# One kernel, three edits: adaLN's later vectors summed along rows, w_out rounded on ScalarE, the output projection's store moved

## The chip, the cores and the metric

The kernel runs on one core of one Trainium2 chip. The metric is the device time of one execution in microseconds (us). Engines are named as the profile names them: PE is TensorE's matmul side and PEld its weight loads, DVE is VectorE, ACT is ScalarE, POOL is GpSimd, SP is SyncE, which here only issues transfers.

## What is computed

One layer of an encoder trunk with batch 1, sequence 1024 and width 1024, all in float32. A conditioning vector c gives six vectors of 1024 numbers (adaLN), which modulate the layer:

```python
mod = silu(c) @ w_ada + b_ada                      # 6 vectors: shift, scale, gate for each half
h = modulate(rms_norm(x), shift_mix, scale_mix)
proj = h @ w_in                                    # q, k, v of 8 + 8 heads of 64
oa = chunked_rel_attention(...)                    # 8 heads, a band of 9 chunks of 64
ob = stick_breaking_attention(...)                 # 8 heads, causal, cumulative products
x = x + gate_mix * (concat(rms_norm(oa) * g_a, rms_norm(ob) * g_b) @ w_out)
h = modulate(rms_norm(x), shift_ffn, scale_ffn)
gate, val = split(causal_depthwise_conv(h @ w_up))
x = x + gate_ffn * ((silu(gate) * val) @ w_down)   # then a last rms_norm
```

Vectors 0 and 1 (shift_mix, scale_mix) are needed at the start. The "later vectors" are 2 to 5: gate_mix for the output projection, shift_ffn and scale_ffn for the second half, gate_ffn for its last product.

## The kernel before, in words

Every float32 product is made of three products of rounded parts: each operand is split into a high part (the value rounded to fp32r) and a low part (the rest), and `mm3g` (L468) issues high by high, high by low, low by high.

The work has three stages: a prologue to about 60 us (rms_norm, vectors 0 and 1 by `ada_sum` at L250, the first q and k), the attention to about 640 us, and the feed-forward part to the end.

The attention is one list of 128 units (L939): 8 pairs of heads, 4 groups of queries, 2 heads, 2 blocks of 128 queries. Units 0 to 63 are stick-breaking: scores, two sigmoids, a scan on VectorE (L799), a product on POOL (L802). Units 64 to 127 are chunked attention: scores, a maximum on VectorE (L767, L771), exp on ScalarE (L778), normalisation on POOL (L795). Then TensorE transposes the probabilities (tile T from pb), ScalarE and VectorE split them (L821, L822), and TensorE multiplies them by v. The loop at L944 works two units ahead with the scores, and between these steps `fill` (L664) puts in matmuls of a list of jobs with due times (L609 to L652): the q, k and v projections of coming pairs, then `job_out_b` (L545), the half of the output projection that belongs to the stick-breaking heads, and two blocks of `job_out_a`. By the planner's costs and due times `job_out_b` begins in unit 106 and ends in unit 125.

At the end of each unit from MOD0 = 60 on (L48, L972) the loop takes one step of `mods` (L891). One step handles two tiles of w_ada, 128 inputs by 256 outputs each (tile rawm, four buffers, loads at L901). VectorE multiplies a tile by one value of silu(c) per partition and adds it to macc (L916, L918). There are 4 vectors by 4 quarters by 8 tiles, 128 tiles. After each eighth tile `mod_out` (L924) sums macc over the partitions with TensorE: for vectors 3 and 4 two products of macc by a column of ones (shown as T<-ones,macc), for the gates one product of ones by macc (T<-macc,ones), into a PSUM buffer that the transposes use too (T, three buffers). A gate's quarter gets its bias from a small load and is stored to the scratch gate_d, from where `load_gate` (L542) reads it back broadcast.

Four things set the order. TensorE's instructions are pinned to the order of the program (`pe`, L134 to L136). The other engines' instructions and SP's transfers are put in order by the framework's scheduler, which goes by program order and by its own model of when a thing is ready; each engine then runs its list strictly in that order, and an instruction that waits holds all behind it. All transfers are issued by SP. And a buffer is refilled only when its last reader is done.

`job_out_b` works on 16 blocks of 128 rows by 512 columns. For one block it loads the rows of x, issues 12 matmuls, scales the result on VectorE (L567), adds it to x on POOL (L568), and stores it to scratch tb_d (L569). `load_wout` (L516) loads a tile of w_out, rounds it on VectorE (L521) and takes the rest on POOL (L522); two buffers (raw) hold the loads. The lines around a block's end are:

```python
yield from mm3g(ps, out_prs(wo, ot, tb, hf, fbs), 216)      # L565
ve.scalar_tensor_tensor(st, ps, rB[:, tb:tb + 1], bc[:, cc], ALU.mult, ALU.mult)
gp.tensor_add(xt, xt, st)
sy.dma_start(tb_d[tb, :, cc], xt)                           # L569
```

`mm3g` gives control back after each matmul, the last one too; there is no such point between L566 and the next block's first matmul.

Of the kernel before, what the change touches and what calls it, by code (L numbers as in the profile page):

```python
# [47 lines left out]
MOD0 = 60  # L48
# [7 lines left out]
def build(nc, tc, t, ctx):  # L56
# [3 lines left out]
    def mk(pool, shape, dt, tag):  # L60
        cnt[0] += 1
        return pool.tile(shape, dt, name=f"{tag}_{cnt[0]}", tag=tag, bufs=BUFS.get(tag, 1))
# [16 lines left out]
    rev_d = mk(dr, [8, P, ULEN], F32, "revd")  # L79

# [54 lines left out]
    def pe(fn, *a, **k):  # L135
# [7 lines left out]
    smask = mk(pq, [P, P], F32, "smask")  # L143
    gp.memset(smask, 0.0)
    gp.affine_select(out=smask, in_=smask, pattern=[[-1, P]], compare_op=ALU.is_gt,
                     fill=NEG, base=0, channel_multiplier=1)
    smaskr, identr = (mk(pq, [P, P], F32R, n) for n in ("smaskr", "identr"))
    gp.tensor_copy(smaskr, smask)
# [69 lines left out]
    ada = t["ada0"]  # L218
    sh_mix = mk(p0, [P, KB], F32, "sh_mix")
# [235 lines left out]
    sy.dma_start(rev_d, bass.AP(t["rev"].tensor, 0, [[ULEN, 8], [0, P], [1, ULEN]]))  # L455
    new_k(pairs[0])
# [59 lines left out]
    def load_wout(kb, hf):  # L516
        cc = slice(hf * HALF, (hf + 1) * HALF)
        raw = load_w(t["w_out"][kb, :, cc], [P, HALF])
        wh = mk(pH, [P, HALF], F32R, "H")
        wl = mk(pH, [P, HALF], F32R, "H")  # L520
        ve.tensor_copy(wh, raw)  # L521
        gp.tensor_sub(wl, raw, f(wh))  # L522
        return wh, wl
# [21 lines left out]
    def job_out_b(_):  # L545
# [10 lines left out]
        bc = mk(p1, [P, S + 1], F32, "kt")  # L556
        load_gate(bc[:, 0:D])
        gate.append(bc)
        for hf in range(2):
            cc = slice(hf * HALF, (hf + 1) * HALF)  # L560
            for tb in range(TB):
                ps = mk(ps1, [P, HALF], F32, "mm")
                xt = mk(p0, [P, KB, P], F32, "wh").rearrange("p a b -> p (a b)")[:, 0:HALF]
                sy.dma_start(xt, t["x"][tb * P:(tb + 1) * P, cc])
                yield from mm3g(ps, out_prs(wo, ot, tb, hf, fbs), 216)  # L565
                st = mk(p0, [P, KB, P], F32, "wl").rearrange("p a b -> p (a b)")[:, 0:HALF]  # L566
                ve.scalar_tensor_tensor(st, ps, rB[:, tb:tb + 1], bc[:, cc], ALU.mult, ALU.mult)  # L567
                gp.tensor_add(xt, xt, st)  # L568
                sy.dma_start(tb_d[tb, :, cc], xt)  # L569
                if hf == 1 and tb == 3:  # L570
                    for fb in range(4):
                        ot[fb, 0] = load_o(fb, 0, fb < 3)
                    for fb in range(4):
                        wo[fb, 0] = load_wout(fb, 0)
        for fb in range(4):
            wo[fb, 1] = load_wout(fb, 1)
# [312 lines left out]
    QC = 256  # L889

    def mods():  # L891


        seq = [(i, qt, kb) for i in MODS for qt in range(D // QC) for kb in range(KB)]
        tiles = {}

        def load(n):
            if n < len(seq):
                i, qt, kb = seq[n]
                tiles[n] = mk(p1, [P, QC], F32, "rawm")  # L900
                sy.dma_start(tiles[n], t["ada"][i - 2, kb, :, qt * QC:(qt + 1) * QC])  # L901

        load(0)
        load(1)
        yield
        for n, (i, qt, kb) in enumerate(seq):
            cols = i in (3, 4)
            if n % 2 == 0:
                load(n + 2)
                load(n + 3)  # L910
            w = tiles.pop(n)
            if kb == 0:
                if cols and qt == 0:
                    modv[i] = mk(p0, [P, KB], F32, f"mod{i}")
                acc = mk(p1, [P, QC], F32, "macc")
                ve.tensor_scalar(acc, w, cact[:, 0:1], None, ALU.mult)  # L916
            else:
                ve.scalar_tensor_tensor(acc, w, cact[:, kb:kb + 1], acc, ALU.mult, ALU.add)  # L918
            if kb == KB - 1:
                mod_out(i, qt, acc, cols)  # L920
            if n % 2:
                yield

    def mod_out(i, qt, acc, cols):  # L924
        mp = mk(ps1, [P, HALF], F32, "T")
        if cols:
            for b in range(2):
                pe(te.matmul, mp[:, b:b + 1], acc[:, b * P:(b + 1) * P], ones[:, 0:1], start=True, stop=True)
            k0 = 2 * qt
            ve.scalar_tensor_tensor(modv[i][:, k0:k0 + 2], mp[:, 0:2], 0.0 if i == 3 else 1.0,  # L930
                                    bada[:, 8 * i + k0:8 * i + k0 + 2], ALU.add, ALU.add)
        else:
            pe(te.matmul, mp[:, 0:QC], ones, acc, start=True, stop=True)
            bb = mk(p1, [1, QC], F32, "rawm")
            sy.dma_start(bb, bass.AP(t["b_ada"].tensor, i * D + qt * QC, [[QC, 1], [1, QC]]))
            ve.tensor_add(acc[0:1], mp[0:1, 0:QC], bb)
            sy.dma_start(gate_d[i // 5:i // 5 + 1, qt * QC:(qt + 1) * QC], acc[0:1])
# [583 lines left out]
```

## Time and profile before

| | us |
|---|---|
| median of 3 runs | 1426.35 |
| lowest and highest run | 1421.34, 1428.23 |
| the profiled execution, its own time | 1425.51 |
| its span, first to last instruction | 1423.5 |
| busy in it: PE, DVE, POOL, ACT | 1309.2, 1176.2, 864.9, 617.2 |

The profile is one execution, recorded instruction by instruction. Busy time of an engine says how much it did, not whether the end waited for it. A wait is idle time of an engine together with what ended it. Matmuls are pipelined, so the time between the starts of two of them is less than the duration shown. PEclk is the TensorE clock that was granted, as a share of 2.4 GHz; its two levels are 1.2 and 2.4 GHz, so 0.5 would be the lower level throughout.

### The profile page before, as it was taken

Reading aid. Unit: us, or ns where it says so; the run is one execution under the profiler, and the core shown is the slowest. Engines: PE = TensorE matmul, PEld = TensorE weight load, DVE = VectorE, ACT = ScalarE, POOL = GpSimd, SP = SyncE. Lnnn points to the kernel's source line nnn. Section 1 sums busy time; section 2 is a strip of 40 time slices with the busy share of each in tenths; the row PEclk is TensorE's granted clock in tenths of the full one; section 3 lists DMA queues with packets and bytes.
Section 4 is the critical chain, followed back from the end, with each engine's and each line's share of the span. In section 5 each row is a group of like instructions: output and inputs, shape, how many; then the busy total and the mean of one; then the engine's idle time right before and its main releaser. Section 6 shows DMA issues by size and latency. Waiting matters only on the chain.

```text
span 1423.5 us, 19845 instructions
## 1 busy us (share of the span) xinstructions
PE 1309.2 (92%) x6644; PEld 1083.0 (76%) x6644; DVE 1176.2 (83%) x1967; ACT 617.2 (43%) x1270; POOL 864.9 (61%) x760
## 2 busy tenths in 40 slices
PE   4889999999899978798887999999999999999996
PEld 2688998898778966676665877777777778777774
DVE  7858777677778868876889889999998889899887
ACT  5647567575545433333432333323333333333334
POOL 4646576765333436563578667776676677667664
PEclk9999999999999999899998999999999999999998
DMA  8534433414665686665011111111111111211213
GB/s 311 180 100 112 104 88 85 119 49 120 166 167 144 179 263 197 217 193 193 22 45 36 47 52 45 45 45 60 52 54 58 45 45 45 60 52 49 62 37 119
DMA packets 80047, 144.57 MB, mean 102 GB/s; under 512 B 10041, under 2 KB 36809, under 8 KB 79946
## 3 DMA queue, kind: packets, MB, share of 16 engines
q1 hardware_dynamic: 79946, 143.31, 33.9%
q8 instruction: 53, 0.87, 0.3%
q14 instruction: 48, 0.39, 0.1%
HBM read 102.89 MB, written 18.88 MB: 86 GB/s over the span
## 4 chain that ended last, share of the span: by engine, by line
PE 43%; DVE 35%; ACT 7%; issue 5%; DMA 5%; POOL 4%; SPq 1%; POOLq 0%; DVEq 0%; ACTq 0%
PE mm L136 14%; PE up L1128 12%; DVE y L1137 8%; PE T L136 6%; PE dnf L136 6%; DVE x L1262 4%; PE S L136 3%; ACT y L1133 3%; DVE ah L1071 3%; DVE y L1070 2%; DVE adaw L254 1%; DVE macc L918 1%; PE up L1302 1%; POOL wl L121 1%; DVE al L1072 1%
## 5 line engine op out<-in xcount | busy, mean ns | idle before, releaser
L1262 DVE TENSOR_TENSOR x<-dnf,x 128x512 f32<-128x512 f32 x340 | 222.5, 679 | 1.6 <-PE dnf L136 1.6
L1137 DVE SCALAR_TENSOR_TENSOR y<-y,sm,y 128x512 f32<-128x512 f32 (+2 forms) x160 | 187.3, 1171 | 28.8 <-ACT y L1133 28.7
L1128 PE MATMUL up<-h,wh 128*128 128x512 f32 x640 | 199.7, 393 | 2.6 <-ACT y L1170 1.8
L1094 POOL TENSOR_TENSOR wl<-raw,wh 128x1024 fp32r<-128x1024 f32 (+1 forms) x62 | 160.1, 2583 | 66.1 <-ACT wh L1092 59.5
L1133 ACT ACTIVATE y<-y,sm 128x512 f32<-128x512 f32 x80 | 65.3, 817 | 254.7 <-DVE y L1209 133.4
L136 PE MATMUL mm<-H,wh 128*128 128x512 f32 x448 | 150.2, 403 | 0.0
L1128 PEld LDWEIGHTS up<-h,wh 128*128 128x128 f32 x640 | 119.7, 189 | 31.1 <-ACT y L1170 5.2
L136 PE MATMUL dnf<-dh,ah 128*128 128x512 f32 x336 | 133.5, 397 | 10.0 <-DVE x L1262 8.8
L136 PE MATMUL dnf<-dl,ah 128*128 128x512 f32 x336 | 134.0, 399 | 3.7 <-POOL dl L1240 2.5
L802 POOL TENSOR_TENSOR pb<-pb,kt 128x512 f32<-128x512 f32 (+2 forms) x96 | 89.4, 945 | 77.0 <-DVE kt L799 50.0
L136 PE MATMUL dnf<-dh,al 128*128 128x512 f32 x336 | 132.6, 395 | 0.9 <-DVE al L1072 0.9
L1128 PE MATMUL up<-h,wl 128*128 128x512 f32 x320 | 125.3, 392 | 0.0
L822 DVE TENSOR_TENSOR ptl<-T,pth 128x512 fp32r<-128x512 f32 (+2 forms) x192 | 98.5, 517 | 30.7 <-ACT pth L821 29.0
L821 ACT CAST pth<-T 128x512 fp32r<-128x512 f32 (+2 forms) x192 | 87.4, 457 | 62.3 <-PE T L136 60.9
L795 POOL TENSOR_SCALAR pb<-pb,ri 128x640 f32<-128x640 f32 (+2 forms) x64 | 45.4, 711 | 106.2 <-DVE ri L794 67.7
L136 PE MATMUL mm<-wh,H 128*128 128x256 f32 x512 | 102.8, 292 | 6.6 <-DVE vs L511 6.6
L799 DVE TENSOR_TENSOR_SCAN kt<-kt 128x128 f32<-128x128 f32 (+3 forms) x64 | 98.2, 1534 | 9.8 <-ACT kt L784 9.4
L1128 PE MATMUL up<-Tc,wh 128*128 128x512 f32 x320 | 100.9, 396 | 4.6 <-ACT y L1154 4.5
L1240 POOL TENSOR_TENSOR dl<-modt,dh 128x512 fp32r<-128x512 f32 x42 | 65.3, 1554 | 64.3 <-ACT dh L1239 64.3
L1237 POOL TENSOR_TENSOR modt<-modt,modt 128x512 f32<-128x512 f32 x44 | 68.8, 1563 | 58.2 <-DMA modt<-w_down 58.2
L136 PE MATMUL S<-kh,qs 128*128 128x384 f32 (+5 forms) x352 | 99.5, 364 | 4.6 <-ACT pb L778 4.4
L136 PE MATMUL T<-ident,pb 128*128 128x128 f32 x528 | 91.1, 277 | 8.8 <-POOL pb L802 3.5
(214 smaller groups left out, 3451.1 us busy)
## 6 DMA issues: line engine op xcount, KB each, us to landing
raw<-w_up SPq DMA_DIRECT2D x44, 512.0 KB, 3.6
rawm<-ada SPq DMA_DIRECT2D x128, 128.0 KB, 2.4
qs<-ex SPq DMA_DIRECT2D x104, 128.0 KB, 2.5
modt<-w_down SPq DMA_DIRECT2D x44, 256.0 KB, 2.7
adaw<-ada SPq DMA_DIRECT2D x16, 512.0 KB, 5.7
raw<-w_qk SPq DMA_DIRECT2D x16, 512.0 KB, 3.6
kh<-ex SPq DMA_DIRECT2D x56, 128.0 KB, 2.6
tbd<-wh SPq DMA_DIRECT2D x18, 256.0 KB, 2.6
```

Source lines behind the costliest of these rows:

```text
L136: r = fn(*a, **k)
L799: ve.tensor_tensor_scan(r, r, r, 1.0, ALU.mult, ALU.bypass)
L802: gp.tensor_mul(pt[:, a:b], pt[:, a:b], kt[:, a + 1:b + 1])
L821: sc.copy(dh, tp[:, 0:b - a])
L822: ve.tensor_sub(dl, tp[:, 0:b - a], f(dh))
L1094: late.append(lambda a=a, z=z: ko(gp.tensor_sub(wl[:, a:z], raw[:, a:z], f(wh[:, a:z]))))
L1128: ko(te.matmul(ps, w[x][:, kb], b[kb][y], start=start and n == 0, stop=n == 11, skip_group_check=True))
L1133: ko(sc.activation(y[:, a:z], src[:, a:z], AF.Identity, scale=cw[2][:, b], bias=cb[:, b]))
L1137: ko(ve.scalar_tensor_tensor(y[:, o:z], src[:, o - d:z - d], cw[2 - d][:, b], y[:, o:z], ALU.mult, ALU.add))
L1237: ko(gp.tensor_mul(raw, raw, gbc[hf]))
L1240: ko(gp.tensor_sub(wl, raw, f(wh)))
L1262: r = ve.tensor_add(xc, ps, xc)
```

## The change

The later vectors are no longer summed over the partitions. The host hands w_ada over transposed, with 128 outputs on the partitions and the inputs along the row. silu(c), which the prologue has as a row on every partition, is stored once to scratch c_d and read back broadcast, half a row at a time (tile chalf, one buffer). One VectorE instruction (tensor_tensor_reduce, the form of L254) multiplies a tile of 128 by 512 by it and sums along the row into one column of asum. There are 2 halves by 4 vectors by 8 tiles, 64 tiles, one a step, with two buffers; a vector is complete when its second half is, gate_mix with the 40th tile. `mod_out` adds the halves and the bias in two instructions of 8 columns and stores a gate with one transfer of 128 by 8 single elements. MOD0 goes from 60 to 50. `job_out_b` would take further steps of `mods` by itself if gate_mix were not there yet. `load_wout` rounds on ScalarE. A block's store is written behind the allocation of the next block's PSUM tile. The scratch for the causal mask moves to a pool that is closed after the prologue.

```diff
--- before.py
+++ after.py
@@ -38,14 +38,14 @@
 BUFS = {
     "raw": 2, "wh": 3, "wl": 3, "H": 32, "adaw": 3, "xs": 8, "modt": 3, "mod0": 2,
     "qs": 8, "kh": 4, "ex": 2, "vs": 3, "nm": 4, "rs": 4, "ri": 4,
-    "pb": 3, "kt": 2, "oth": 2, "otl": 2, "o": 1, "fx": 1, "pth": 3, "ptl": 3, "rawm": 4, "sq": 1, "msr": 2, "e0": 2,
+    "pb": 3, "kt": 2, "oth": 2, "otl": 2, "o": 1, "fx": 1, "pth": 3, "ptl": 3, "rawm": 2, "sq": 1, "msr": 2, "e0": 2,
     "a0": 4, "w0": 4, "t0": 3, "mm": 2, "S": 3, "T": 3, "T2": 2, "dn": 2, "dnf": 4, "up": 4,
     "x2": 8, "h2": 32, "y": 4, "ah": 2, "al": 2, "dh": 2, "dl": 2, "Tc": 24,
 }
 AHEAD = 2
 TR = 3
 T2A, T2B = 6, 2
-MOD0 = 60
+MOD0 = 50
 FILL = 2, 2, 0, 0
 MODS = 2, 3, 4, 5
 EARLY = 2
@@ -77,6 +77,7 @@
     tb_d = mk(dr, [TB, P, D], F32, "tbd")
     gate_d = mk(dr, [2, D], F32, "gated")
     rev_d = mk(dr, [8, P, ULEN], F32, "revd")
+    c_d = mk(dr, [1, D], F32, "cd")
 
     c0, p0 = pool("p0", side="left")
     ident = mk(p0, [P, P], F32, "ident")
@@ -140,12 +141,7 @@
     hT = [[(mk(pH, [P, HALF], F32R, "H"), mk(pH, [P, HALF], F32R, "H")) for _ in range(2)] for _ in range(KB)]
     cq, pq = pool("pq", side="right", reuse_waits="tile")
     lo64, hi64 = slice(0, HD), slice(HD, P)
-    smask = mk(pq, [P, P], F32, "smask")
-    gp.memset(smask, 0.0)
-    gp.affine_select(out=smask, in_=smask, pattern=[[-1, P]], compare_op=ALU.is_gt,
-                     fill=NEG, base=0, channel_multiplier=1)
     smaskr, identr = (mk(pq, [P, P], F32R, n) for n in ("smaskr", "identr"))
-    gp.tensor_copy(smaskr, smask)
     gp.tensor_copy(identr, ident)
 
     def halves(h):
@@ -216,6 +212,11 @@
     cps0, ps0 = pool("ps0", space=PSUM)
     cs, pst = pool("pst", side="right", reuse_waits="tile")
     ada = t["ada0"]
+    smask = mk(pst, [P, P], F32, "smask")
+    gp.memset(smask, 0.0)
+    gp.affine_select(out=smask, in_=smask, pattern=[[-1, P]], compare_op=ALU.is_gt,
+                     fill=NEG, base=0, channel_multiplier=1)
+    gp.tensor_copy(smaskr, smask)
     sh_mix = mk(p0, [P, KB], F32, "sh_mix")
     sc_mix = mk(p0, [P, KB], F32, "sc_mix")
 
@@ -453,6 +454,7 @@
     first_mm(7, [1])
     split_v0(1)
     sy.dma_start(rev_d, bass.AP(t["rev"].tensor, 0, [[ULEN, 8], [0, P], [1, ULEN]]))
+    sy.dma_start(c_d, cbc[0:1])
     new_k(pairs[0])
     for hf in range(2):
         evac_q0(acc0[0][hf], hf, pairs[0].qs)
@@ -518,7 +520,7 @@
         raw = load_w(t["w_out"][kb, :, cc], [P, HALF])
         wh = mk(pH, [P, HALF], F32R, "H")
         wl = mk(pH, [P, HALF], F32R, "H")
-        ve.tensor_copy(wh, raw)
+        sc.copy(wh, raw)
         gp.tensor_sub(wl, raw, f(wh))
         return wh, wl
 
@@ -554,24 +556,30 @@
         for fb in fbs:
             wo[fb, 1] = load_wout(fb, 1)
         bc = mk(p1, [P, S + 1], F32, "kt")
+        while not gate_up:
+            next(bg)
         load_gate(bc[:, 0:D])
         gate.append(bc)
+        store = None
         for hf in range(2):
             cc = slice(hf * HALF, (hf + 1) * HALF)
             for tb in range(TB):
                 ps = mk(ps1, [P, HALF], F32, "mm")
+                if store:
+                    sy.dma_start(*store)
                 xt = mk(p0, [P, KB, P], F32, "wh").rearrange("p a b -> p (a b)")[:, 0:HALF]
                 sy.dma_start(xt, t["x"][tb * P:(tb + 1) * P, cc])
                 yield from mm3g(ps, out_prs(wo, ot, tb, hf, fbs), 216)
                 st = mk(p0, [P, KB, P], F32, "wl").rearrange("p a b -> p (a b)")[:, 0:HALF]
                 ve.scalar_tensor_tensor(st, ps, rB[:, tb:tb + 1], bc[:, cc], ALU.mult, ALU.mult)
                 gp.tensor_add(xt, xt, st)
-                sy.dma_start(tb_d[tb, :, cc], xt)
+                store = tb_d[tb, :, cc], xt
                 if hf == 1 and tb == 3:
                     for fb in range(4):
                         ot[fb, 0] = load_o(fb, 0, fb < 3)
                     for fb in range(4):
                         wo[fb, 0] = load_wout(fb, 0)
+        sy.dma_start(*store)
         for fb in range(4):
             wo[fb, 1] = load_wout(fb, 1)
         for fb in range(4):
@@ -886,55 +894,44 @@
     later = []
     modv = {}
 
-    QC = 256
+    asum = mk(p0, [P, 2, len(MODS), KB], F32, "asum")
+    gate_up = []
 
     def mods():
 
 
-        seq = [(i, qt, kb) for i in MODS for qt in range(D // QC) for kb in range(KB)]
-        tiles = {}
-
-        def load(n):
-            if n < len(seq):
-                i, qt, kb = seq[n]
-                tiles[n] = mk(p1, [P, QC], F32, "rawm")
-                sy.dma_start(tiles[n], t["ada"][i - 2, kb, :, qt * QC:(qt + 1) * QC])
+        seq = [(hf, n, kb) for hf in range(2) for n in range(len(MODS)) for kb in range(KB)]
+        tiles, ch = {}, {}
+
+        def load(x):
+            if x < len(seq):
+                hf, n, kb = seq[x]
+                cc = slice(hf * HALF, (hf + 1) * HALF)
+                if n == 0 and kb == 0:
+                    ch[hf] = mk(p1, [P, HALF], F32, "chalf")
+                    sy.dma_start(ch[hf], bass.AP(c_d.tensor, c_d.offset + hf * HALF, [[0, P], [1, HALF]]))
+                tiles[x] = mk(p1, [P, HALF], F32, "rawm")
+                sy.dma_start(tiles[x], t["ada"][n, kb, :, cc])
 
         load(0)
-        load(1)
         yield
-        for n, (i, qt, kb) in enumerate(seq):
-            cols = i in (3, 4)
-            if n % 2 == 0:
-                load(n + 2)
-                load(n + 3)
-            w = tiles.pop(n)
-            if kb == 0:
-                if cols and qt == 0:
-                    modv[i] = mk(p0, [P, KB], F32, f"mod{i}")
-                acc = mk(p1, [P, QC], F32, "macc")
-                ve.tensor_scalar(acc, w, cact[:, 0:1], None, ALU.mult)
-            else:
-                ve.scalar_tensor_tensor(acc, w, cact[:, kb:kb + 1], acc, ALU.mult, ALU.add)
-            if kb == KB - 1:
-                mod_out(i, qt, acc, cols)
-            if n % 2:
-                yield
-
-    def mod_out(i, qt, acc, cols):
-        mp = mk(ps1, [P, HALF], F32, "T")
-        if cols:
-            for b in range(2):
-                pe(te.matmul, mp[:, b:b + 1], acc[:, b * P:(b + 1) * P], ones[:, 0:1], start=True, stop=True)
-            k0 = 2 * qt
-            ve.scalar_tensor_tensor(modv[i][:, k0:k0 + 2], mp[:, 0:2], 0.0 if i == 3 else 1.0,
-                                    bada[:, 8 * i + k0:8 * i + k0 + 2], ALU.add, ALU.add)
-        else:
-            pe(te.matmul, mp[:, 0:QC], ones, acc, start=True, stop=True)
-            bb = mk(p1, [1, QC], F32, "rawm")
-            sy.dma_start(bb, bass.AP(t["b_ada"].tensor, i * D + qt * QC, [[QC, 1], [1, QC]]))
-            ve.tensor_add(acc[0:1], mp[0:1, 0:QC], bb)
-            sy.dma_start(gate_d[i // 5:i // 5 + 1, qt * QC:(qt + 1) * QC], acc[0:1])
+        for x, (hf, n, kb) in enumerate(seq):
+            load(x + 1)
+            w = tiles.pop(x)
+            ve.tensor_tensor_reduce(out=w, in0=w, in1=ch[hf], scale=1.0, scalar=0.0, op0=ALU.mult, op1=ALU.add,
+                                    accum_out=asum[:, hf, n, kb:kb + 1])
+            if hf and kb == KB - 1:
+                mod_out(n, MODS[n])
+            yield
+
+    def mod_out(n, i):
+
+        v = modv[i] = mk(p0, [P, KB], F32, f"mod{i}")
+        ve.tensor_add(v, asum[:, 0, n], asum[:, 1, n])
+        ve.scalar_tensor_tensor(v, v, 1.0 if i == 4 else 0.0, bada[:, 8 * i:8 * i + KB], ALU.add, ALU.add)
+        if i in (2, 5):
+            sy.dma_start(bass.AP(gate_d.tensor, gate_d.offset + i // 5 * D, [[1, P], [P, KB]]), v)
+            gate_up.append(i)
 
     units = [Unit(p, g, h, u) for p in range(NP) for g in range(4) for h in range(2) for u in range(2)]
     parts = {}
@@ -1493,7 +1490,7 @@
     w_up, conv_w = np.asarray(w_up), np.asarray(conv_w)
     w6 = w_ada[0].reshape(KB, P, 6, D)
     ada0 = w6[:, :, 0:2].reshape(D, 2, KB, P).transpose(2, 3, 1, 0)
-    ada = w6[:, :, 2:6].transpose(2, 0, 1, 3)
+    ada = w_ada[0].T.reshape(6, KB, P, D)[2:6]
     wi = w_in[0].reshape(KB, P, 2, 3, 4, P)
     wi = wi[:, :, ::-1]
     w_qk = wi[:, :, :, 0:2].transpose(2, 4, 3, 1, 0, 5).reshape(NP, 2, P, KB, P)
```

## Rows read from the trace of the kernel before

**Rows 1.** Stretches: length, busy us of each engine (instructions), PEclk, DMA share, GB/s
```profile
320.00:640.00 320.00, 285.02 (x1691) 246.28 (x1690) 255.89 (x757) 141.31 (x400) 150.35 (x183) 0.95 0.64 183
...
240.00:320.00 80.00, 78.38 (x514) 70.58 (x514) 60.71 (x82) 54.09 (x130) 55.68 (x76) 1.00 0.33 85
...
400.00:420.00 20.00, 16.95 (x92) 14.34 (x91) 14.31 (x48) 6.42 (x21) 5.62 (x11) 0.91 0.70 179
...
580.00:600.00 20.00, 11.52 (x60) 9.75 (x58) 18.54 (x41) 5.95 (x18) 13.36 (x13) 0.83 0.68 213
600.00:620.00 20.00, 19.41 (x103) 16.04 (x104) 14.83 (x47) 6.64 (x20) 6.94 (x7) 0.92 0.49 147
```

**Rows 2.** TensorE's waits, 320 to 640 us: us in total, times, longest
```profile
PE T L136 <- DVE macc L918: 11.8, 3, 6.6
PE S L136 <- ACT pb L778: 6.6, 5, 2.3
PE mm L136 <- DVE H L521: 6.1, 2, 3.6
...
PE T L136 <- DVE mod L930: 0.6, 1, 0.6
```

**Rows 3.** Timeline of TensorE; columns: start us, us, instructions, [idle before, its releaser]
```profile
411.40 0.58 PE L136 MATMUL T<-ones,macc 128*128 128x1 f32 x4 [3.05 <-DVE macc L918]
...
507.50 0.50 PE L136 MATMUL T<-ones,macc 128*128 128x1 f32 x4
507.86 0.59 PE L136 MATMUL S<-kh,qs 128*128 128x384 f32 x2
...
559.11 1.19 PE L136 MATMUL T<-macc,ones 128*128 128x256 f32 x2 [2.17 <-DVE macc L918]
...
573.56 0.65 PE L136 MATMUL T<-macc,ones 128*128 128x256 f32 x2
573.86 0.81 PE L136 MATMUL S<-kh,qs 128*128 128x512 f32 x2
...
600.31 1.19 PE L136 MATMUL T<-macc,ones 128*128 128x256 f32 x2 [6.59 <-DVE macc L918]
```

**Rows 4.** Busy time of the instructions on tile macc alone, by stretch
```profile
320.00:640.00 320.00, 10.46 (x48) 7.15 (x48) 73.45 (x128) 0.95 0.64 183
60.00:320.00 260.00, 0.00 (x0) 0.00 (x0) 4.78 (x8) 0.99 0.36 94
```

**Rows 5.** Instructions of L254 and of L771; ns min/median/max, first and last start us
```profile
L254 DVE CUSTOM_DVE_ANT_0 adaw<-adaw,cbc x16: 1209/1212/2309, 18.2 to 55.4; 128x1024 f32<-128x1024 f32 x16
L254 DVE DVE_READ_ACCUMULATOR2_ANT sh_mix<- x8: 76/78/83, 19.3 to 55.0; 128x1 f32 x8
...
L771 DVE CUSTOM_DVE_ANT_0 S<-S,kt x64: 285/432/433, 332.9 to 626.8; 128x256 f32<-128x256 f32 x56, 128x128 f32<-128x128 f32 x8
L771 DVE DVE_READ_ACCUMULATOR2_ANT nm<- x64: 82/141/144, 333.1 to 627.1; 128x1 f32 x64
```

**Rows 6.** The instructions on tile rawm; columns as in rows 5
```profile
L918 DVE SCALAR_TENSOR_TENSOR macc<-rawm,cact,macc x112: 414/485/1594, 76.9 to 620.0; 128x256 f32<-128x256 f32 x112
...
DMA to landing us min/median/max: 2.1/2.4/5.5
```

**Rows 7.** Groups by line and form: busy us, mean ns, idle before and releaser
```profile
L1092 ACT CAST wqh<-raw 128x512 fp32r<-128x512 f32 x20 | 12.1, 606 | 0.0
...
L521 DVE CAST H<-raw 128x512 fp32r<-128x512 f32 x16 | 10.9, 688 | 2.1 <-DMA raw<-w_out 2.1
```

**Rows 8.** Instructions of L799, the scan of the stick-breaking units
```profile
L799 DVE TENSOR_TENSOR_SCAN kt<-kt x64: 408/1520/2690, 85.3 to 328.2; 128x128 f32<-128x128 f32 x8, 128x256 f32<-128x256 f32 x8, 128x384 f32<-128x384 f32 x8, 128x512 f32<-128x512 f32 x8
```

**Rows 9.** The page's main DMA queue: packets, MB, share of 16 engines' span
```profile
q1 hardware_dynamic: 79946, 143.31, 33.9%
```

**Rows 10.** What SyncE's queue waited for, 320 to 640 us
```profile
SPq L569 <- POOL wh L568: 31.2, 15, 4.0
```

**Rows 11.** What VectorE waited for, 320 to 640 us
```profile
DVE macc L918 <- DMA rawm<-ada: 7.5, 6, 4.7
```

## The prediction

> **What bounds the kernel now.** I read the busy time by stretch first, because the change acts in one stage. From 320 to 640 us, where the chunked units run, the output projection begins and nearly all of the later vectors' work lies, PE is busy 285.0 of 320 us and DVE 255.9, at a mean granted clock of 0.95 [rows 1]. From 240 to 320 PE is busy 78.4 of 80 at full clock, and from 580 to 600 only 11.5 of 20 while DVE is busy 18.5 [rows 1]. So PE's pinned order is the bound, and in the later stage DVE now and then keeps it standing. The view of PE's waits says for what: the longest item is macc, 11.8 us in 3 waits; then come scores that wait for the exp (6.6), the rounded w_out (6.1), and 0.6 behind L930 [rows 2]. PE's timeline shows the three: 3.05 us at 411, 2.17 at 559 and 6.59 at 600 us, each ahead of a `mod_out` product [rows 3]. After such a wait PE runs for some microseconds at the lower of its two levels, 1.2 GHz: the stretches behind the first and the third have a clock of 0.91 and 0.92 [rows 1].
>
> **The change part by part.** The sum is made on the profiled execution, 1425.51 us, 0.84 below the median of the runs.
>
> **Matmuls of mod_out, removed.** Spacing of starts, not duration, is what they take: from a group of four ones,macc to the next matmul 507.86 - 507.50 = 0.36 us, from a pair macc,ones to the next 573.86 - 573.56 = 0.30 [rows 3]. Eight groups and eight pairs make 2.9 + 2.4 = 5.3 us. Their busy time, 10.5 us [rows 4], counts overlap and is the upper end. They also leave the buffers T to the transposes. I take -5.3.
>
> **PE's waits for macc and L930, removed.** 11.8 + 0.6 = 12.4 us [rows 2]. What is late next is work on the same DVE: scores that wait for the maximum and exp, transposes that wait for their split. So not all of it comes back; ends 0 and -12.4. I take two thirds, -8.3, since scores and probabilities run two units ahead and were rarely late themselves (6.6 us in 5 waits).
>
> **The lower clock behind them.** 20 us at 0.91 and 20 at 0.92 lose 1.8 + 1.6 = 3.4 us [rows 1]. Ends 0 and -3.4; I take -2.
>
> **DVE's sums, replaced.** The old ones took 73.5 us in the stage and 4.8 before it [rows 4]. The new form is not in the trace at 512 columns. L771, the same instruction, takes 432 ns at 256 columns and 285 at 128, so about 0.7 us at 512; L254 takes 1,212 at 1,024, and less a slope of some 0.53 per 512 that is 0.68 [rows 5]. Its accumulator is read by a second instruction, 78 to 141 ns [rows 5]. 64 x (0.70 + 0.14) = 54 us is the lower end. L918 lasts 414 ns at best and 1,594 at worst [rows 6], and L254 1,209 and 2,309 [rows 5]: something holds such instructions up. If every new one were stretched as the worst L254 was, it would be 64 x (0.70 x 1.9 + 0.14) = 94 us, the upper end. The nearest row is L918, whose median of 485 lies 71 ns above its best; I take twice that and a little, 0.18 each, and 64 x 1.02 = 65 us. At the upper end DVE would get no relief in the stage, and the -4 below would be 0.
>
> The Trainium skill (SBUF — State Buffer, Who interferes with whom) says that a DVE instruction with two SBUF inputs and a POOL instruction that reads SBUF exclude each other, and that the later one waits out the whole of the other. The spread of L918 and L254 agrees. By it the new sums, longer each, would hold POOL 0.7 us at a time, but half as often, so it changes no sign.
>
> **The earlier start.** Ten of 64 tiles, 10 us of DVE, go to units 50 to 59, before 320 us. What is left in the stage is 54 x 1.02 = 55 us against 73.5.
>
> **w_out on ScalarE.** 16 x 0.688 = 11.0 us leave DVE, and 16 x 0.605 = 9.7 us come to ACT by the nearest row, L1092 at 512 columns [rows 7]; ACT is busy 141 of 320 us [rows 1], which hides them. An ACT copy whose load is late holds the exps and evictions behind it; DVE's own waits for w_out came to 2.1 us [rows 7].
>
> DVE's stage thus goes from 255.9 to 255.9 - 18 - 11 = 227 us, 71% of it rather than 80%. Waits of PE that hang on DVE or on the rounding come to 6.6 + 6.1 [rows 2]; ends 0 and -12.7. The w_out waits partly remain, as they start with a late load. I take -4.
>
> **What units 50 to 59 pay.** The scan of a late stick-breaking unit takes up to 2.69 us and its last ends at 328 us [rows 8]. DVE goes there from 60.7 to 70.9 of 80 us while PE has 1.6 us idle [rows 1]. A sum that starts just ahead of a scan delays it by 1 us, and with it the product on POOL and the transposes. Ends 0 and +10; I take +2, since units are two ahead.
>
> **New transfers.** The second half of silu(c) has one buffer, so its load waits for the 32nd tile and the 33rd tile for it: once, at most the longest landing of rawm, 5.5 us [rows 6]. The two gate stores are 1,024 single elements each. A packet of the main queue took on average 0.339 x 16 x 1423.5 / 79,946 us = 97 ns [rows 9], for 1.8 KB; as an estimate 1,024 such packets over 16 engines take at most 6.2 us each time. They lie under other work (gate_mix is complete in unit 90, `job_out_b` begins in 106), and can only make a tile late. Ends 0 and +18, I take +1. The small stores and bias loads that go, eight each, were as hidden: 0.
>
> The Trainium skill (DMA: Bandwidth & Descriptors, Rules for kernel authors) says that a transfer whose last dimension is not contiguous becomes one descriptor per element, and advises against it. No row here shows such a transfer; by that rule the sum stays as it is, as the count above already takes one packet per element.
>
> **The store.** It is said to come one block later. In the code nothing gives up control between L566 and the next block's first matmul, so store, load of x and first matmul still come in the same order and the store still waits for POOL's addition of its own block. Only after block 4 of the second half do ten loads come ahead of it in the program. SP's wait at L569, 31.2 us in 15 times [rows 10], stays: 0. The mask's move puts three POOL instructions behind one: 0.
>
> **Sum.** -5.3 - 8.3 - 2 - 4 + 2 + 1 = -16.6, so 1408.9 in a profiled execution and **1409.7** as a median.
>
> **The rivals.**
>
> *The place is taken (0.20).* PE leaves macc and stands at the next thing that DVE owes. For it: DVE is the busy one just where PE stands, 18.5 of 20 us [rows 1]. Against: after the change the sums end by unit 114, and this stretch lies at about 115 to 120. Then only the matmuls and little else come back: 1426.35 - 5.3 + 1 = 1422.
>
> *Late tiles, the slower side (0.10).* With two buffers of twice the size only one tile is ahead, as its load must wait for the sum before the last. Where SP is held (up to 4.0 us [rows 10]), the load comes late, and the sum stands at the head of DVE with the maxima and splits of the units behind it. Before, 6 such waits took 7.5 us [rows 11], 1.25 each. If all 64 waited so, DVE would stand 80 us against the 29 it is relieved of. It decides from about 30 us of such waits on. At 80, the 51 us beyond the relief fall on DVE's idle time (64 us) and on PE; a third of it on PE makes 17, and with PE's gain from waits gone: 1426.35 + 17 - 5.3 + 2 = 1440. Against: a unit lasts (626.8 - 332.9) / 63 = 4.7 us [rows 5], twice the median landing of 2.4 [rows 6].
>
> *All of it comes back (0.12).* Waits, clock and DVE's relief at their full ends: -5.3 - 12.4 - 3.4 - 10 + 1 = -30, 1396.
>
> *The store does move (0.05).* If the scheduler placed it behind the next loads, SP would be free earlier and w_out and tiles earlier with it; half of the 6.1 us more [rows 2]: 1407.
>
> **How the numbers follow.** The forecast has 0.53. Its own range is 1400 to 1419. All of it together: the full end of the gains puts the low bound at 1395, the taken place with the upper bounds of the new costs the high one at 1430; outside lies most of the slower case and a little of the best, under 2 in 10. Within 0.5%, about 7 us, cannot be told from no change: faster ends at 1419. Faster: 0.50 of the forecast, 0.12, 0.05 and 0.05 of the taken place, 0.72. Same: 0.03 + 0.13 = 0.16. Slower: 0.10 + 0.02 = 0.12.
>
> **What would show it.** Right: no PE wait named after the sums; 64 sums of about 0.7 to 1 us, 65 us in all; PE's clock near 1 around 400 and 600 us; the start of the feed-forward stage some 15 us earlier and its length unchanged; SP's wait at the store about 31 us as before. Wrong: PE's idle time in the chunked units unchanged with other names on it (place taken), or DVE standing for rawm over 30 us in all (late tiles), or new waits of PE for the product of L802 before 330 us.

## The result, and the profile after

The changed kernel takes 1440.87 us (median of 4 runs, 1439.88 to 1442.71) against 1423.85 for the kernel before (4 runs by then): a ratio of 1.0118, 95% interval 1.0085 to 1.015. The forecast was 1409.7, so it is on the other side. The profiled execution took 1439.88 us, 14.4 more than that of before.

Where the time went shows in the busy time by stretch of the changed kernel (columns as in [rows 1]):

```profile
60.00:320.00 260.00, 212.93 (x1304) 185.50 (x1303) 194.41 (x340) 131.31 (x315) 134.07 (x182) 0.93 0.50 139
320.00:640.00 320.00, 305.65 (x1928) 270.61 (x1927) 224.71 (x646) 176.30 (x484) 167.35 (x223) 0.98 0.49 136
```

From 320 to 640 us PE is busier, 305.7 us against 285.0 [rows 1], at a clock of 0.98 against 0.95. This is not the gain that was forecast: the stretch is fixed in time, and in it PE also does what the stage before left undone (1,928 matmuls against 1,691). The loss is in that stage before, of which the same view of the kernel before says:

```profile
60.00:320.00 260.00, 249.65 (x1656) 226.65 (x1655) 185.61 (x267) 165.09 (x397) 160.90 (x231) 0.99 0.36 94
```

PE was busy 36.7 us less there, and 20.6 us more behind it. The DMA share went up from 0.36 to 0.50: something is loaded there that was loaded later before. The list of instructions on tile rawm in the changed kernel says what (columns as in rows 5; the last two lines: what VectorE waited for ahead of it, us and times, and the time from issue to landing of its loads):

```profile
L914 SPq DMA_DIRECT2D rawm<-ada x64: 327/330/692, 71.9 to 267.1; - x64
L921 DVE CUSTOM_DVE_ANT_0 rawm<-rawm,chalf x64: 660/693/1582, 77.1 to 270.3; 128x512 f32<-128x512 f32 x64
...
  DMA rawm<-ada: 37.1, 25
...
DMA to landing us min/median/max: 2.4/2.8/13.0
```

All 64 sums, which the program puts at the ends of units 51 to 114 (the first step, in unit 50, only loads), run from 77 to 270 us, among the scans of the stick-breaking units. The old ones began early too, at 76.9 us [rows 6], but only 8 of them: the other 128 instructions on macc lay behind 320 us [rows 4]. In VectorE's list all 64 new sums stand ahead of the 38th scan of 64: four before the first scan, then up to three between two scans, 1.7 a unit. At this pace the two buffers are not refilled in time: VectorE stands at the head of its list for tiles, 37.1 us in 25 times, and what is queued behind comes late to PE. PE's waits from 60 to 320 us (columns as in rows 2), of the changed kernel:

```profile
PE T L137 <- DVE ptl L830: 26.4, 15, 9.2
PE mm L137 <- DVE vs L513: 7.8, 4, 6.4
PE T L137 <- POOL pb L810: 7.4, 4, 3.6
```

None of these names the sums. The split of the transposed probabilities (ptl) and the product behind the scan (pb) are the work that stands behind them on VectorE and POOL. In the kernel before, the items of this stretch came to some 10 us, nearly all in these two:

```profile
PE mm L136 <- DVE vs L511: 6.6, 1, 6.6
PE T L136 <- POOL pb L802: 3.5, 3, 1.6
```

From 320 to 640 us PE's longest item is now 4.2 us, where it was 11.8 for macc [rows 2].

The first up product of the feed-forward part (L1302 before, L1299 after) starts at 701.5 us; the list of its instructions in the changed kernel, then in the kernel before:

```profile
L1299 PE MATMUL up<-h,wh x128: 387/389/775, 701.5 to 778.8; 128*128 128x512 f32 x128
L1302 PE MATMUL up<-h,wh x128: 387/389/775, 686.3 to 762.9; 128*128 128x512 f32 x128
```

This start is 15.2 us later, which covers all the 14.4 by which the profiled executions differ.

**The longest of the waits** has a cause of its own. Lines of the timeline of the changed kernel, first SP's, then VectorE's, then TensorE's (columns as in rows 3):

```profile
201.17 0.39 SPq L933 DMA_DIRECT2D gated<-mod  x1
...
206.25 0.27 DVE L513 TENSOR_TENSOR vs<-mm,vs 128x128 fp32r<-128x128 f32 x1
214.87 0.69 DVE L921 CUSTOM_DVE_ANT_0 rawm<-rawm,chalf 128x512 f32<-128x512 f32 x1 [8.35 <-DMA rawm<-ada]
...
216.97 1.09 PE L137 MATMUL T<-ident,pb 128*128 128x128 f32 x4 [9.19 <-DVE ptl L830]
```

The first gate store, 1,024 single elements, is issued at 201.17 us and the next tile right behind it. That tile lands after 13.0 us, where the median is 2.8. VectorE stands 8.35 us for it and PE 9.19. In the same stretch, by windows:

```profile
203.00:213.00 10.00, 4.33 (x30) 3.47 (x28) 3.32 (x7) 3.01 (x9) 2.40 (x5) 0.92 0.27 15
213.00:218.00 5.00, 1.03 (x5) 1.06 (x6) 3.13 (x6) 0.00 (x0) 0.00 (x0) 0.50 0.48 144
```

For 10 us the transfers move 15 GB/s. After its stand PE has the lower of its two levels, 1.2 GHz. The packets from 202 to 203 us and from 203 to 213 us, and the two gate stores with their median time from issue to landing:

```profile
DMA packets 1048, 0.02 MB, mean 21 GB/s; under 512 B 1040, under 2 KB 1040, under 8 KB 1048
DMA packets 74, 0.15 MB, mean 15 GB/s; under 512 B 1, under 2 KB 1, under 8 KB 74
gated<-mod SPq DMA_DIRECT2D x2, 4.0 KB, 11.4
```

The single elements are thus through by 203 us, but the store lands only 11.4 us after its issue, and until then the packets of the tile behind it come slowly. What holds them in these 10 us the trace does not show.

### The profile page after: what moved, and what is told of

It is laid out like the page before. It is cut to its first block, busy times and chain, and to the rows that moved or that the text cites. A ratio compares the mean times of both kernels' runs of the same rounds, so it can differ in the third digit from the quotient of the medians.

```text
span 1438.1 us, 19575 instructions
## 1 busy us (share of the span) xinstructions
PE 1309.9 (91%) x6596; PEld 1080.2 (75%) x6596; DVE 1161.6 (81%) x1943; ACT 623.1 (43%) x1286; POOL 864.7 (60%) x760
## 4 chain that ended last, share of the span: by engine, by line
DVE 39%; PE 35%; DMA 8%; ACT 7%; issue 5%; POOL 4%; SPq 1%; POOLq 0%; DVEq 0%; ACTq 0%
PE up L1125 12%; PE mm L137 11%; DVE y L1134 9%; PE dnf L137 6%; PE T L137 5%; DMA rawm<-ada 5%; DVE x L1259 4%; ACT y L1130 3%; DVE kt L807 3%; DVE ah L1068 2%; DVE y L1067 2%; PE S L137 2%; DVE rawm L921 2%; DVE ptl L830 2%; DVE adaw L255 1%
## 5 line engine op out<-in xcount | busy, mean ns | idle before, releaser
L810 POOL TENSOR_TENSOR pb<-pb,kt 128x512 f32<-128x512 f32 (+2 forms) x96 | 93.7, 989 | 111.9 <-DVE kt L807 69.4
L137 PEld LDWEIGHTS T<-ident,pb 128*128 128x128 f32 x528 | 66.5, 143 | 51.0 <-issue 25.6
```

The lines of the kernel that those rows point to most:

```text
L137: r = fn(*a, **k)
L810: gp.tensor_mul(pt[:, a:b], pt[:, a:b], kt[:, a + 1:b + 1])
```

## The experiments

The theory: the sums' order costs the time, since they run ahead into the stick-breaking stage, faster than their tiles can come. Rivals: the rounding on ScalarE costs it; the sums cost it by their length, wherever they stand; the tiles' loads cost it through DMA alone. All ratios are to the kernel before, run on the same chip beside them, whose medians lay between 1422 and 1425 us.

**The rounding** (alone in the kernel before; and taken back in the changed one).

```diff
-        ve.tensor_copy(wh, raw)
+        sc.copy(wh, raw)
```

> The kernel before with the rounding of w_out on ScalarE alone. Theory A: 0 to 5 us faster than before (1419 to 1425), PE's waits for the rounded w_out shorter. Theory B: slower by some of the 17 us, 1428 to 1440.

> The changed kernel with the rounding of w_out back on VectorE. Theory A: 0 to 5 us slower than the changed kernel, 1440 to 1446. Theory B: faster than it by over 5 us, under 1436.

Alone it gives 1414.69 us, 0.9933 [0.9914, 0.9951], some 10 us of gain. Taken back in the changed kernel, the time is 1439.59, 1.0098 [1.0081, 1.0115], as with it. So it is no cause of the loss. Its gain alone was larger than the 0 to 5 us expected, and the waits for the rounded w_out, which were to be shorter, are as long as before. PE's waits from 320 to 640 us in this run, beside [rows 2], show macc down from 11.8 to 6.9 us; that VectorE is less loaded where macc was late is the likely reason, and was not tried. The profiled execution is the slowest of the four, 7.0 us under that of before:

```profile
PE S L136 <- ACT pb L778: 7.4, 6, 2.9
PE T L136 <- DVE macc L918: 6.9, 3, 3.0
PE mm L136 <- ACT H L521: 6.0, 2, 4.4
```

**No sums at all.** The changed kernel without loads and sums, asum set to zero (these parts of the vectors are left out).

```diff
-        load(0)
+        gp.memset(asum.rearrange('p a b c -> p (a b c)'), 0.0)
...
-            load(x + 1)
-            w = tiles.pop(x)
-            ve.tensor_tensor_reduce(out=w, in0=w, in1=ch[hf], ...
```

> The changed kernel without the sums of the later vectors and without the loads of their tiles (the later vectors are the bias alone). Theory A: the floor of everything that these sums cost, 1385 to 1405 us. Theory B: what else the change brought is still there, 1420 or more.

1379.02 us, 0.9682 [0.9664, 0.97]: 61.9 us under the changed kernel, and faster than the 1385 to 1405 expected. This bounds all that sums and loads can cost.

**Sums tied to their units.** One word more, and the framework keeps the sum in the order of the program.

```diff
-            ve.tensor_tensor_reduce(out=w, in0=w, in1=ch[hf], ...
+            ko(ve.tensor_tensor_reduce(out=w, in0=w, in1=ch[hf], ...
```

> The changed kernel with one addition: each of the 64 sums is tied in program order to the VectorE instruction traced before it, so it stays in its unit (50 to 113). Theory A (the sums ran ahead into the stick-breaking stage because nothing ties them to a unit, and VectorE there stood 37 us for their tiles): 1400 to 1415 us, PE busy about 250 us between 60 and 320 us as before the change, waits of VectorE for rawm under 10 us. Theory B (another part of the change costs the time: the rounding on ScalarE, the copy of silu(c), the moved mask): stays at 1435 to 1445. Theory C (the sums cost as much wherever they stand, as each holds VectorE longer): 1425 to 1440, with PE's lost time between 320 and 600 us.

1413.62 us, 0.9921 [0.9905, 0.9937]: 27.3 us come back with nothing but the order changed. In this run, the list of instructions on rawm and the window of the stick-breaking stage:

```profile
L921 DVE CUSTOM_DVE_ANT_0 rawm<-rawm,chalf x64: 666/685/1631, 286.2 to 564.0; 128x512 f32<-128x512 f32 x64
...
  DMA rawm<-ada: 5.9, 5
...
60.00:320.00 260.00, 249.73 (x1659) 225.41 (x1659) 185.67 (x273) 164.86 (x396) 164.32 (x230) 0.99 0.36 99
```

The sums now begin at 286 us, PE's 249.7 us are those of before, and tile waits are 5.9 us.

> Sums tied to units 50 to 113, w_out rounded on VectorE: the first edit alone, without its running ahead. If the two gains are of one kind (both relieve VectorE in the same units, and the rounding on ScalarE already took it): 1414 to 1419, close to the run with both (1413.6). If the tied sums gain nothing by themselves, the rounding on ScalarE is the whole gain: 1422 to 1428.

Tied sums with the rounding back on VectorE: 1412.1, 0.9918 [0.99, 0.9935], faster than the 1414 to 1419 expected. So the rounding brings 10 us by itself, the tied sums 11.5 by themselves, and both together 11.3. Both relieve VectorE in the stage where PE waits for it; that they save the same waits was argued, not tried.

**What held the old sums?** The kernel before, with the products and the PSUM buffer of `mod_out` taken out and copies in their place (the sum over partitions is left out).

```diff
-        mp = mk(ps1, [P, HALF], F32, "T")
...
-            pe(te.matmul, mp[:, 0:QC], ones, acc, start=True, stop=True)
...
-            ve.tensor_add(acc[0:1], mp[0:1, 0:QC], bb)
+            ve.tensor_add(acc[0:1], acc[0:1], bb)
```

> The kernel before, with the old sums, but without their products over the partitions on TensorE and the PSUM buffer these take (a sum's end is copied within VectorE, so the later vectors are not the reference's). The scheduler's list then has all 128 old sums ahead of the 46th scan. Theory A: what was lost in the change was this tie, so the old sums lose as much without it: 1432 to 1450, VectorE standing over 25 us for rawm before 320 us, although 5 us of matmuls and 12 of waits are gone. Rival (the new form or its tiles of 256 KB are the cause): 1405 to 1420, faster than before.

1437.23 us, 1.0107 [1.0092, 1.0123]: the old sums without their matmuls lose as the new ones do. Instructions and window of this run:

```profile
L918 DVE SCALAR_TENSOR_TENSOR macc<-rawm,cact,macc x112: 452/485/1368, 76.4 to 307.1; 128x256 f32<-128x256 f32 x112
...
60.00:320.00 260.00, 213.12 (x1299) 185.19 (x1298) 216.93 (x345) 130.76 (x313) 126.40 (x181) 0.95 0.48 137
```

All sums are done by 308 us instead of 620 [rows 6], and PE is busy 213.1 us in the stage, as in the changed kernel. VectorE waits 24.7 us there for tiles and the gates' small transfers (15.0 + 6.5 + 3.2 by the list of instructions on macc); the part for rawm, 18.2, is less than the 25 expected. So it was the product over the partitions, with the buffer T that it shares with the transposes, that tied the old sums: 8 tiles could run ahead, then macc had to wait for its product. With the products kept but not pinned to TensorE's order, a program that was built and not run, VectorE's list still has 8 sums early and 120 behind the scans; that it is the buffer rather than the pin is read from this list alone. MOD0 has no part in the loss: with MOD0 = 60 the changed kernel's lists on all engines and on SP are the same (built, not run).

**Where they start, when tied.** From the first unit (MOD0 = -2), from unit 20, and one step in every second unit.

```diff
-MOD0 = 50
+MOD0 = -2
```

> The sums tied to their units as in the first experiment, but from unit -2 on, one a unit, so they stand in the stick-breaking stage about as the free ones do in the changed kernel (these went from 77 to 270 us). Theory A1 (the cost is the place: between scans VectorE has too little room, and a sum at the head of its list waits for its tile): 1430 to 1445, PE busy 215 to 235 of 260 us from 60 to 320. Theory A2 (the cost is the running ahead of its own loads alone, one a unit leaves each tile a unit's time): 1405 to 1418, VectorE's waits for rawm under 10 us.

> The sums tied to units 20 to 83, one a unit, half among the scans and half among the chunked units. If the start hardly matters as long as there is one a unit: 1408 to 1416, as from unit -2 (1411.5) and from unit 50 (1413.6). If the place matters, one outside of that.

> Sums tied to their units, one every second unit from -2 to 128, so half of them stand among the scans and none closer than two units. Theory: the cost of a sum grows with what stands with it in its unit, and a tile has two units to land: 1398 to 1410. Rival: what a sum costs is its time on VectorE wherever it stands, or the late end (unit 128) makes the second half wait: 1411 or more.

1411.47, 1415.23 and 1415.95 us; 0.9909 [0.989, 0.9929], 0.9945 [0.993, 0.996] and 0.9939 [0.9918, 0.996]. At one a unit or less the stage hardly matters for the total: in the first of these runs PE is busy 235.6 us from 60 to 320 us against 249.7 when tied from unit 50, and makes it good behind. One in every second unit was expected at 1398 to 1410 if two units' time to land helped; it did not. Sums among the scans thus cost no more by themselves than sums among the chunked units.

**Density and loads.** Tied, but with as many sums in each unit as the changed kernel has there; and the two paces without loads (sums read one tile of zeros, the vectors' values are left out).

```diff
-        if i >= MOD0:
+        for _ in range(STEPS.get(i, 0)):
             next(bg, None)
```

> The sums tied to units, but as densely as the free ones stand in the changed kernel (64 sums by the 38th scan, 1.7 a unit, up to 3 in one). Theory A3 (what costs is the density: the tiles cannot land in time when two or three are due in a unit and two buffers hold them): 1430 to 1445, VectorE standing over 25 us for rawm. Rival (the free order costs in another way, not through place or density): 1405 to 1420.

> The same dense order, every sum on one tile of zeros, no tile of w_ada and no half of silu(c) loaded (the later vectors are the bias alone). Theory A3: 1400 to 1412, as the waits for tiles are gone and VectorE's work costs about what it costs at one a unit (1402.5). Rival (VectorE's occupation in these units is the cost): within 8 us of the dense run with loads.

> The kernel of the run from unit -2 on, but every sum reads one tile of zeros, and no tile of w_ada and no half of silu(c) is loaded: the same VectorE work at the same places without a wait for a transfer (the later vectors are the bias alone). If VectorE's occupation is what costs there: within 5 us of the run with loads. If the waits for tiles are: 10 to 25 us under it, 1400 to 1415.

| tied sums | with loads | without loads | difference |
|---|---|---|---|
| one a unit | 1411.47 | 1402.49 | 9.0 |
| dense | 1427.69 | 1408.02 | 19.7 |

Ratios: 0.9909 and 0.985 [0.9835, 0.9865] for one a unit, 1.0028 [1.0016, 1.004] and 0.9892 [0.9876, 0.9909] dense. The dense run lies between the two ranges expected, so density is a part of the loss and not all of it. Density costs 16.2 us with loads and 5.5 without: most of its price comes with the tiles. On rawm, the dense run has VectorE wait

```profile
  DMA rawm<-ada: 30.1, 18
```

us and times. Without loads the sums still cost 1402.5 - 1379.0 = 23.5 us, the price of 64 such instructions on VectorE. The dense tied order is 13.2 us faster than the changed kernel, which has about as many in each unit but spread otherwise between the scans (four ahead of the first scan, where the tied order has none) and 7 us more of tile waits. The traces say where the rest lies: from 60 us to the first up product PE is idle 68.0 us and busy 573.5 in the changed kernel, at a mean clock of 0.96, and idle 62.5 and busy 564.2 in the dense one, at 0.98, for as many matmuls (3,487 and 3,485). So 5.5 us are idle time, and 9.3 are the same matmuls at a lower mean clock. Which difference in the order brings this was not tried.

**The gate store.** The gate's outputs are dealt so that a partition holds 8 neighbours, with the host's layout of w_ada and b_ada to match: 128 runs of 32 bytes instead of 1,024 of 4.

```diff
-            sy.dma_start(bass.AP(gate_d.tensor, gate_d.offset + i // 5 * D, [[1, P], [P, KB]]), v)
+            sy.dma_start(bass.AP(gate_d.tensor, gate_d.offset + i // 5 * D, [[KB, P], [1, KB]]), v)
```

> The changed kernel, but the two gates' outputs lie 8 to a partition (w_ada and b_ada handed over in that order), so a gate is stored as 128 runs of 8 elements rather than 1,024 single ones. The order of the instructions is the same on every engine. If the store holds the tile load behind it (it took 13.0 us to land, the median is 2.8): 1428 to 1434, and no wait of VectorE over 6 us. If it is hidden: 1438 to 1443.

> Sums tied to units from -2 on, one a unit, and gates stored in runs of 8. The store's cost there is smaller, as a tile has a unit's time: 1405 to 1411 (1411.5 without it). If the store matters only in the free order: 1410 to 1413.

In the changed kernel 1432.28, 1.0048 [1.0029, 1.0067]: 8.6 us back, with nothing else in any engine's list altered. The store now lands 2.1 us after its issue instead of 11.4, and VectorE's longest wait for a tile is 6.1 us, where under 6 was expected. With sums tied from the start 1409.62, 0.9894 [0.9878, 0.9911]: 1.9 us less, and the two intervals overlap. On rawm in the first of the two:

```profile
  DMA rawm<-ada: 32.6, 25
...
DMA to landing us min/median/max: 2.4/2.7/8.5
```

**A third tile buffer**, paid with one buffer less of oth and otl, and loads two ahead; in the changed kernel, with sums tied from the start, and the latter with the gate store mended too.

```diff
-            load(x + 1)
+            load(x + 2)
```

> The changed kernel with three buffers for the tiles and a load two ahead (the buffers that hold the attention's output parts go from two to one to make room). If the free order costs because two buffers cannot cover it: 1420 to 1432, VectorE standing under 25 us for rawm. If a third buffer is only filled with a sum still further ahead (the sums run ahead by as much as there are buffers): 1436 or more.

> Sums tied to units from -2 on, one a unit, three buffers, load two ahead, the output parts' buffers at one. The run without any loads was 9 us faster (1402.5): 1403 to 1409 if the tiles' lateness is what those 9 us are; 1410 or more if a deeper prefetch does not reach it, or the single output buffers cost as much.

> Sums tied to units from -2 on, one a unit, three buffers, gates stored in runs of 8. If the two edits add up: 1402 to 1405 (1405.2 and 1409.6 alone, 1411.5 with neither). If the third buffer already covers the gate store: 1404 to 1407.

Free sums: 1425.78, 1.0019 [0.9996, 1.0041], 15.1 us back (ten runs, 1420.30 to 1435.02); tile waits 19.2 us in 17 times instead of 37.1. Tied from the start: 1405.22, 0.986 [0.9845, 0.9874], tile waits 0.5 us. With the mended store **1403.5 us** (1403.37 to 1407.94), 0.9879 [0.9857, 0.9901], 37.4 us under the changed kernel. Beside its own runs of the kernel before it is no better than with the old store (0.986): with three buffers and tied sums no gain of the mended store is shown. Its lines on rawm and its windows:

```profile
L922 DVE CUSTOM_DVE_ANT_0 rawm<-rawm,chalf x64: 656/798/1611, 88.0 to 357.1; 128x512 f32<-128x512 f32 x64
...
  DMA rawm<-ada: 0.8, 1
...
60.00:320.00 260.00, 238.37 (x1545) 213.85 (x1544) 210.33 (x356) 152.27 (x364) 171.57 (x215) 0.97 0.52 148
320.00:640.00 320.00, 302.13 (x1839) 262.66 (x1837) 228.20 (x672) 169.05 (x464) 168.02 (x206) 0.99 0.54 159
```

PE is busy 11 us less than in the kernel before from 60 to 320 us, and 17 us more from 320 to 640 us, at a clock of 0.99 instead of 0.95.

## Why the prediction was wrong

**The step that failed** is "The earlier start": "Ten of 64 tiles, 10 us of DVE, go to units 50 to 59, before 320 us." It took MOD0 for the place where the sums run. But only TensorE is pinned, and the scheduler puts other instructions by its own model of when they are ready. The part "Matmuls of mod_out, removed" counted what these cost (5.3 us) and what they leave free, and didn't ask what they held back. With them went the only tie, and all 64 sums ran ahead. Two runs show it: tying the new sums, with nothing else altered, gains 27.3 us, and untying the old ones, by taking out their products, loses about 15.

**Term by term.** In the order that the sum assumed (tied from unit 50), 1413.6 was measured against the forecast 1409.7: about -11 instead of -16.6 us. It is not made up as forecast either. From 320 us to the first up product, which starts at 686.3 us before and at 674.2 in the tied run (columns as in rows 1; the kernel before first):

```profile
320.00:686.30 366.30, 325.50 (x1879) 277.67 (x1878) 287.37 (x815) 160.76 (x438) 165.95 (x203) 0.96 0.61 179
320.00:674.20 354.20, 314.06 (x1829) 268.09 (x1828) 259.67 (x785) 169.53 (x456) 174.95 (x203) 0.96 0.63 182
```

The stretch is 12.1 us shorter and PE is busy 11.4 us less, but idle as long as before: 40.8 and 40.1 us, by one execution each. (In the tied run with the rounding back on VectorE, PE's idle time from 60 us to this product is 47.4 us against 51.2 before, so a little was won there.)

- "PE's waits for macc and L930", -8.3: gone by name, and hardly in sum. PE's longest waits in the tied run from 320 to 640 us (columns as in rows 2) have other names:

```profile
PE mm L137 <- ACT H L523: 6.8, 2, 4.7
PE S L137 <- ACT pb L786: 6.4, 4, 3.0
PE T L137 <- DVE ptl L830: 4.7, 5, 1.8
PE T L137 <- POOL pb L803: 4.6, 2, 2.9
```

- "Matmuls of mod_out", -5.3: too small. The fall of 11.4 us in PE's busy time is near their busy time, 10.5 us [rows 4], which the prediction called the upper end.
- "The lower clock behind them", -2: the mean clock from 320 to 640 us is 0.96 in the tied run, where it was 0.95 [rows 1].
- The sums' length: right. In the changed kernel the 64 sums take 57.4 us and the reads of their accumulators 5.1, so 62.5 against the 65 taken; in the tied run 51.1 + 5.0. The median, 0.693 us, is near the best case, and the stretched ones make the mean 0.907. The Trainium skill (SBUF — State Buffer, Who interferes with whom) says that a VectorE instruction with two SBUF inputs contends with a POOL instruction that reads SBUF. The trace agrees: all 22 sums over 0.9 us overlap an instruction on POOL, and the 26 that overlap none took 0.695 us at most.
- w_out on ScalarE: 0.621 us each against 0.605 predicted. PE's wait for it did not go, 6.8 us in the tied run against 6.1 [rows 2]; the prediction had said that a part remains. The relief of VectorE was taken as -4 us together; the rounding alone brought 10, and nothing on top of tied sums. What isn't additive was added.
- "New transfers", +1 between 0 and +18: in the changed kernel the gate stores, of single elements, cost 8.6 us; with sums tied from the start the difference was 1.9, within the intervals. The step priced the packets, at 6.2 us a store at most: they went by within the one microsecond from 202 to 203 us, but the store landed after 11.4 us. "They lie under other work" holds for its own reader, and not for the tile issued right behind it on the same queue. The rule of the Trainium skill (DMA: Bandwidth & Descriptors, Rules for kernel authors), one descriptor per element, agrees with the trace: from 202 to 203 us 1,040 of 1,048 packets have under 512 bytes, about the 1,024 elements of one store.
- "What units 50 to 59 pay", +2: not tested as such, as no sums were there. Tied from unit 50 they left PE's stage as it was, 249.7 us busy.
- The store: 0. The move of the store alone in the kernel before leaves all engines' lists and SP's the same (built, not run). SP's wait there fell from 31.2 us [rows 10] to 15.5, where about 31 was forecast, but the load of x right behind it now waits 14.5 us for the store to land, where it waited 3.3: about as much together. In the tied run the two are 9.1 and 22.7. Why the wait moved from one to the other was not tried.

**The rivals.** "Late tiles" had the mechanism, the threshold (30 us of waits; 37.1 came) and the price (1440; 1440.9 came), but at 0.10 and with a wrong ground: it put the waits in the chunked stage, behind SP's waits at the store. And what was held against it, that a unit lasts twice a landing, assumed one sum a unit; there were 1.7. As the sums lay elsewhere the agreement of the price is partly luck. What the prediction named as the sign, "DVE standing for rawm over 30 us in all", is what the profile shows. The last sign came too, waits of PE for the product on POOL before 330 us: 7.4 us against 3.5. "The place is taken" (0.20) could not show in the changed kernel, as its sums lay elsewhere; in the tied run its sign came, "PE's idle time in the chunked units unchanged with other names on it". Its price, 1422, did not: 1413.6.

## What to carry to other kernels

Before costing work that is removed, ask what it held in place: a product that costs PE 5 to 10 us can be the only thing that keeps 64 loads and sums in their stage. Where a scheduler orders instructions, compare the order of the queues of both kernels before any number, and tie background work to its unit if its pace matters; at one tile a unit the loads cost 9 us, at 1.7 they cost 20. A store of single elements is to be judged by the load issued right behind it, and not by its own reader. And a wait that is removed is no gain until PE's idle time has been seen to fall: what was late behind it may take its place.

## What the hardware showed

A store of 4 KB in 1,024 elements landed 11.4 us after its issue, and the 256 KB load issued behind it on the same queue after 13.0 us instead of 2.8, with 15 GB/s moved, although by the trace the elements' own packets went by within 1 us. In 128 runs of 32 bytes it landed after 2.1 us, and the kernel took 8.6 us less. That so small a transfer would reach PE, through a tile and VectorE's strict order, was not expected.
